# Staging the output projection's weights in the recurrent branch instead of the gating branch (two-layer hybrid trunk, one core)

## The chip, the cores and the metric

The kernel runs on one core of a Trainium2 chip. The metric is the device time of one launch in microseconds (us), the median of several runs. TensorE is PE in the profile, VectorE is DVE, ScalarE is ACT, GpSimd is POOL, and SyncE, which here only issues transfers, is SP.

## The reference

Two layers of the same form act on x, 1024 tokens by 1024 features in fp32. With h = RMSNorm(x) and one input projection `proj = h @ w_in` each layer computes three branches:

```python
ya = rg_lru(causal_depthwise_conv(xa, conv_w, conv_b), ...) * silu(ga)   # recurrent, 384 wide
yb = mla(q_lat, kv_lat, k_rope, positions, ...) * silu(gb)               # attention, 384 wide
yc = spatial_gating(u, v, ...) * silu(gc)                                # gating, 256 wide
y  = concatenate([rms_norm(ya, g[:384]), rms_norm(yb, g[384:768]), rms_norm(yc, g[768:])])
x  = x + rms_norm(y @ w_out, post_g)
```

The recurrent branch runs a convolution of width 4 along the tokens, two sigmoid gates per head and the linear recurrence `h[t] = a[t] h[t-1] + b[t]`. The gating branch multiplies u with a mix of the normalised v inside blocks of 128 tokens.

## The kernel before, in words

Every matrix product is done at fp32 accuracy with three matmuls. Both operands are split in two parts, `hi` (a rounded copy, made on ACT) and `lo` (what the copy misses, a subtraction on DVE or POOL); `mm3` (L126 to L128) adds hi·hi, hi·lo and lo·hi into one PSUM bank. So each weight takes the same road: a transfer from HBM into a slot (SP, L377 for w_in), the `hi` copy on ACT (L386), the `lo` subtraction on POOL or, for the u and v weights, on DVE (L387).

Slots come from a pool called `FS`: seven tiles F_136 to F_142, each 128 x 1024, and the rows of the tile Y while the branch that owns them does not need them. `take` hands out the slot that has been free longest in the program's text; a transfer into a re-used slot waits until the last reader of that slot is done, and SP issues its transfers in order, so one that waits for its slot holds up all that stand behind it.

A layer runs in this order. **Recurrent stage**: `group(g, half)` computes 256 features of xa and ga for one half of the tokens, runs the convolution (ACT L446, DVE L451 and L454) or the gate (ACT L422, DVE L424), and calls `drain(3)`, which issues three pending steps of the recurrence (`lru_steps`: DVE L485 to L509, ACT L473 to L492; the scan is L504). **u and v tokens**: eight tiles of 128 tokens against 512 columns in four weight parts, Gelu on ACT (L687, L690), statistics on DVE (L688). **Gate tokens**: eight tiles against 256 columns (ACT L717, DVE L718). **Latents**: eight tiles against 352 columns, then the gate of the attention branch (ACT L422, DVE L424), loading and scaling the weights w_uq (SP L821, DVE L824). **Attention**, then the **output projection**.

The output projection needs w_out in hi and lo form. `stage_wo` prepares all eight pieces of 128 x 1024 early: load to a slot (SP, L626), for k of 5 or more a scaling on ACT (L630), the split (ACT L367, POOL L368), and two stores to HBM buffers, `wo_dram`: hi on ACT's queue (L632), lo on POOL's queue (L633). The attention loads them back later.

Inside these stages a scheduler chooses each engine's order from its own cost estimates; each engine then runs its list in that order.

Of the kernel before, what the change touches and what calls it, by code (L numbers as in the profile page):

```python
# [8 lines left out]
F32R = mybir.dt.float32r  # L9
BF16 = mybir.dt.bfloat16  # L10
I32 = mybir.dt.int32
AF = mybir.ActivationFunctionType
# [12 lines left out]
W_ROWS = (0, 128, 256, 768, 896, 384, 512, 640)  # L25
# [64 lines left out]
def trunk_kernel(tc, A, out):  # L90
    nc = tc.nc
    keep = tc.keep_in_program_order
    V, S_, G, PE = nc.vector, nc.scalar, nc.gpsimd, nc.tensor
# [20 lines left out]
    def bank(kind):  # L114
        turn[kind] = (turn[kind] + 1) % len(banks[kind])
        return banks[kind][turn[kind]]
# [38 lines left out]
    par = cst.tile([128, 80], F32, name="par")  # L155
# [13 lines left out]
    FS = Slots(cst, NF, 1024, F32, "F")  # L169
# [8 lines left out]
    wo_dram = [[dram.tile([128, 1024], F32, name=f"wo{k}{c}") for c in "hl"] for k in range(8)]  # L178
# [187 lines left out]
    def split(src, h, lo, eng=None):  # L366
        S_.activation(h, src, AF.Copy)  # L367
        (eng or G).tensor_tensor(out=lo, in0=src, in1=h.bitcast(F32), op=ALU.subtract)  # L368
# [148 lines left out]
    def drain(n=1):  # L517
        for _ in range(n):
            if pend:
                pend.pop(0)()  # L520
# [39 lines left out]

    for l in range(DEPTH):

        xc, last, gw = {}, [], []

        def group(g, half):
            pss = [bank("PF") for m in range(2)]
            if g == 0:

                for p in range(2):
                    for m in range(2):  # L570
                        feat(pss[m], hT, ws[g], m, half, slice(p * 256, (p + 1) * 256))
            for m in range(2):
                f = 2 * g + m
                ps = pss[m]
                if g:
                    feat(ps, hT, ws[g], m, half)
                if f < 3:
                    if half == 0:
                        xc[f] = FS.take((128, 1024))
                    conv(l, f, half, ps, xc[f])  # L580
                    if half == 1:
                        steps = lru_steps(l, f, xc[f], gw)
                        pend.extend(steps[:-1])
                        last.append(steps[-1])
                else:
                    gate_in(ps, YA + f - 3, half)
                drain(3)
                if l == 0 and (g, half, m) == (0, 1, 0):
                    softplus_consts()
            if half == 1:  # L590
                ws[g].give()
# [24 lines left out]
        pend.extend(last)  # L616
        pend.append(lambda: [RS.give(t) for t in gw])

        staged = {}

        def stage_wo(n):

            k, r = n // 2, W_ROWS[n // 2]
            if n % 2 == 0:
                staged[k] = FS.take((128, 1024)), FS.take((128, 1024))
                nc.sync.dma_start(out=staged[k][0], in_=A["w_out"][l, r:r + 128, :])  # L626
                return
            st, hi = staged.pop(k)
            if k >= 5:
                S_.activation(st, st, AF.Copy, scale=bgain(r // 128))  # L630
            split(st, hi.bitcast(F32R), st.bitcast(F32R), G)
            S_.dma_start(out=wo_dram[k][0], in_=hi)  # L632
            G.dma_start(out=wo_dram[k][1], in_=st)  # L633
            FS.give(st)
            FS.give(hi)


        for r in yrow[3:5]:
            FS.retire(r)
        vg, ug, gg = [], [], []  # L640

        def bgain(j):
            return par[:, 48 + l * 8 + j:49 + l * 8 + j]

        sg = HS.take((128, 2, 256))
        nc.sync.dma_start(out=sg[:, 0], in_=A["sgu_norm_g"][l].partition_broadcast(128))
# [34 lines left out]
        for t in range(NT):  # L681
            if t % 4 == 0:
                vg.append(FS.take((128, 4, 256)))
                ug.append(FS.take((128, 4, 256)))
            ps = toks(hT, w, t, 512, "P8")
            v = vg[t // 4][:, t % 4]
            S_.activation(v, ps[:, 256:512], AF.Gelu_apprx_tanh)  # L687
            V.bn_stats(out=bst[:, t], in_=v)  # L688
            V.bn_aggr(out=mv[:, t], in_=bst[:, t])
            S_.activation(ug[t // 4][:, t % 4], ps[:, 0:256], AF.Gelu_apprx_tanh)  # L690
            if t == 3:
                pend.extend([lambda: sgu_norm(0), lambda: sgu_affine(0)])
            drain(2)
            stage_wo(t)
        w.give()
        drain(100)
        sw = HS.take((128, 4, 128))
# [14 lines left out]
        for t in range(NT):  # L712
            if t % 4 == 0:
                gg.append(FS.take((128, 4, 256)))
            ps = toks(hT, w, t, 256, "PK")
            th = HS.take((128, 256))
            S_.activation(th, ps[:, 0:256], AF.Tanh, scale=0.5)  # L717
            V.scalar_tensor_tensor(out=gg[t // 4][:, t % 4], in0=th, scalar=1.0, in1=ps[:, 0:256],  # L718
                                   op0=ALU.add, op1=ALU.mult)
            HS.give(th)  # L720
            drain(2)
            stage_wo(8 + t)
        w.give()
        drain(100)
        HS.give(sg)
# [46 lines left out]
        for t in range(NT):  # L772
# [16 lines left out]
            r = rsqrt(ms, 2)  # L789
# [3 lines left out]
            if t % 4 == 3:  # L793
                half = t // 4
                hs = slice(half * 512, (half + 1) * 512)
                for b in range(3):
# [8 lines left out]
                    for r0, n, h, r1, lo in todo:  # L805
                        hi = h[r0:r0 + n, hs]
# [32 lines left out]
        st = FS.take((128, 768))  # L839
# [224 lines left out]
        for n in range(len(units)):  # L1064
# [4 lines left out]
            if n >= len(units) - 4 and n % 2:  # L1069
                half = units[n][1] // 2  # L1070
# [18 lines left out]
        for t in range(NT):  # L1089
# [12 lines left out]
            r = row_rsqrt([z], cols)  # L1102
# [5 lines left out]
            if l + 1 < DEPTH:  # L1108
# [5 lines left out]
                else:  # L1114
# [5 lines left out]
                    n = YS.take((128, 2, 512))  # L1120
# [31 lines left out]
```

## Time and profile before

| | |
|---|---|
| median of 3 runs | 922.84 us (922.6 to 928.7) |
| the profiled execution | 925.49 us, span 923.7 us |
| PE busy | 874.6 us (95%) |
| DVE, ACT, POOL busy | 567.4, 519.5, 426.3 us (61, 56, 46%) |
| mean granted TensorE clock | 0.986 |
| moved over DMA | 86.92 MB |

PE busy 95% of the span leaves 49 us in which it does nothing. In the page's table of 40 slices of 23.1 us POOL shows 0 in the fourth and fifth (69 to 115 us) and in the 23rd and 24th (508 to 554 us): these lie in the recurrent stages of the two layers.

### The profile page before, as it was taken

How to read it: one execution, taken by the hardware profiler on the slowest of the kernel's cores; microseconds unless marked ns; L12 is line 12 of the kernel's file. 1: busy time of each engine (PE TensorE's matmuls, PEld its weight loads, DVE VectorE, ACT ScalarE, POOL GpSimd, SP SyncE). 2: the span in 40 equal slices, each digit the busy share in tenths (PEclk: the TensorE clock that was granted, in tenths of full speed). 3: DMA queues.
4: the chain of work that ended last, by engine and by line, in shares of the span. 5: the costliest groups of instructions: out<-in, count | busy, mean ns of one | idle time of the engine just before them, and what ended most of it. 6: DMA issues, size and time to landing. Idle time of an engine off the chain costs nothing. (4 is left out here: it accounts for less than half of the span.)

```text
span 923.7 us, 13488 instructions
## 1 busy us (share of the span) xinstructions
PE 874.6 (95%) x4982; PEld 768.2 (83%) x4982; DVE 567.4 (61%) x1096; ACT 519.5 (56%) x1032; POOL 426.3 (46%) x469
## 2 busy tenths in 40 slices
PE   4999998999999999989998999999989999899896
PEld 3998787998889888878897888899968888888786
DVE  4567955555599986444465687265446889854322
ACT  6447745554687787445442595353457778755212
POOL 4720056673055767365641002775312467636822
PEclk9999999999999999999999999999989999999998
DMA  7201465412001432123350043762100026201322
GB/s 275 55 25 46 112 220 190 157 64 61 12 1 47 135 126 83 46 71 114 134 152 18 23 111 133 251 222 70 42 7 1 1 58 217 92 23 47 125 103 92
DMA packets 45078, 86.92 MB, mean 94 GB/s; under 512 B 8824, under 2 KB 26836, under 8 KB 45012
## 3 DMA queue, kind: packets, MB, share of 16 engines
q1 hardware_dynamic: 35796, 52.50, 18.5%
q0 software_dynamic: 6912, 25.17, 7.9%
q10 hardware_dynamic: 2304, 8.39, 2.3%
q8 instruction: 39, 0.64, 0.3%
q14 instruction: 27, 0.22, 0.1%
HBM read 60.88 MB, written 25.17 MB: 93 GB/s over the span
## 5 line engine op out<-in xcount | busy, mean ns | idle before, releaser
L126 PE MATMUL pw<-R,R 128*128 128x512 f32 (+1 forms) x704 | 259.7, 370 | 9.4 <-ACT F L1006 3.2
L128 PE MATMUL pw<-R,R 128*128 128x512 f32 (+1 forms) x704 | 252.6, 360 | 1.5 <-POOL R L387 0.8
L127 PE MATMUL pw<-R,R 128*128 128x512 f32 (+1 forms) x704 | 253.1, 360 | 0.0
L126 PE MATMUL pa<-R,R 128*128 128x512 f32 (+3 forms) x540 | 188.6, 352 | 8.5 <-DVE F L718 3.3
L127 PE MATMUL pa<-R,R 128*128 128x512 f32 (+3 forms) x540 | 186.9, 347 | 0.0
L128 PE MATMUL pa<-R,R 128*128 128x512 f32 (+3 forms) x540 | 186.5, 347 | 0.0
L126 PEld LDWEIGHTS pw<-R,R 128*128 128x128 f32 x704 | 134.7, 192 | 32.0 <-ACT F L942 5.9
L128 PEld LDWEIGHTS pw<-R,R 128*128 128x128 f32 x704 | 134.7, 192 | 20.6 <-POOL R L387 1.3
L127 PEld LDWEIGHTS pw<-R,R 128*128 128x128 f32 x704 | 135.0, 192 | 17.1
L126 PEld LDWEIGHTS pa<-R,R 128*128 128x128 f32 x540 | 103.0, 191 | 20.6 <-DVE F L718 3.5
L944 POOL TENSOR_SCALAR F<-F,ring 128x128 f32<-128x128 f32 (+3 forms) x96 | 71.9, 752 | 85.2 <-DVE ring L943 84.0
L128 PEld LDWEIGHTS pa<-R,R 128*128 128x128 f32 x540 | 102.6, 191 | 10.2
L127 PEld LDWEIGHTS pa<-R,R 128*128 128x128 f32 x540 | 103.2, 191 | 9.0
L368 DVE TENSOR_TENSOR R<-pa,R 128x512 fp32r<-128x512 f32 (+1 forms) x120 | 73.8, 629 | 20.9 <-ACT R L367 20.3
L942 ACT ACTIVATE F<-pw,ring 128x128 f32<-128x128 f32 (+3 forms) x96 | 71.0, 741 | 27.3 <-DVE ring L940 25.2
L940 DVE TENSOR_REDUCE ring<-pw 128x1 f32<-128x128 f32 (+3 forms) x96 | 71.7, 748 | 10.7 <-PE pw L128 10.1
L387 POOL TENSOR_TENSOR R<-F,R 128x1024 fp32r<-128x1024 f32 (+1 forms) x24 | 54.2, 2268 | 43.6 <-ACT R L386 43.5
L973 PE MATMUL pa<-R,R 128*128 128x256 f32 x480 | 72.9, 288 | 0.5 <-DVE R L368 0.3
L367 ACT ACTIVATE R<-pa 128x512 fp32r<-128x512 f32 (+1 forms) x120 | 62.9, 553 | 16.4 <-PE pa L964 15.0
L973 PEld LDWEIGHTS pa<-R,R 128*128 128x128 f32 x480 | 64.6, 190 | 3.8 <-DVE R L368 0.5
L964 PE MATMUL pa<-ident,F 128*128 128x128 f32 x432 | 64.4, 274 | 3.5 <-DVE R L368 3.2
L329 ACT ACTIVATE H<-F 128x1024 bf16<-128x1024 f32 (+2 forms) x33 | 31.5, 954 | 55.5 <-DVE F L1008 28.1
(305 smaller groups left out, 1338.7 us busy)
## 6 DMA issues: line engine op xcount, KB each, us to landing
F<-in_w_in SPq DMA_DIRECT2D x24, 512.0 KB, 4.7
F<-in_x SPq DMA_DIRECT2D x13, 512.0 KB, 4.6
F<-in_w_out SPq DMA_DIRECT2D x9, 512.0 KB, 3.5
F<-x SPq DMA_DIRECT2D x8, 512.0 KB, 4.4
Y<-in_w_out SPq DMA_DIRECT2D x7, 512.0 KB, 3.4
x<-F SPq DMA_DIRECT2D x7, 512.0 KB
out_y<-F SPq DMA_DIRECT2D x7, 512.0 KB
Y<-in_w_in SPq DMA_DIRECT2D x6, 512.0 KB, 3.7
```

The source lines that it names most:

```text
L126: PE.matmul(ps, lhsT=sh, rhs=mh, start=start, stop=False)
L127: PE.matmul(ps, lhsT=sh, rhs=ml, start=False, stop=False)
L128: PE.matmul(ps, lhsT=sl, rhs=mh, start=False, stop=stop)
L329: order(S_.activation(q.bitcast(BF16)[:, c], xs[i % len(xs)].rearrange("p a b -> p (a b)")[:, c], AF.Square, scale=1.0 / 32, accum_out=ms[ ...
L367: S_.activation(h, src, AF.Copy)
L368: (eng or G).tensor_tensor(out=lo, in0=src, in1=h.bitcast(F32), op=ALU.subtract)
L387: self.eng.tensor_tensor(out=lo, in0=st, in1=h.bitcast(F32), op=ALU.subtract)
L940: V.tensor_reduce(out=mx, in_=sv, axis=AX.XY, op=ALU.max, negate=True)
L942: S_.activation(p[:, 0:n].rearrange("p (a b) -> p a b", a=sv.shape[1]), sv, AF.Exp, bias=mx, accum_out=sm)
L944: G.tensor_scalar(out=p[:, 0:n], in0=p[:, 0:n], scalar1=rs, scalar2=1.0, op0=ALU.mult, op1=ALU.mult)
L964: PE.transpose(pv[:, c, i * 128:(i + 1) * 128], p[i][:, b * 128:(b + 1) * 128], ident)
L973: PE.matmul(o, lhsT=sv, rhs=pt[:, part, c * 256:(c + 1) * 256], start=(b == 0 and part == 0), stop=(b == nb - 1 and part == 1))
```

## The change

`stage_wo` moves. Before, it is called after each of the eight u and v tokens and after each of the eight gate tokens: the even calls take two slots and load a piece, the odd calls split and store it. Now it is called in `group`, behind `drain(3)`, for nine calls per layer: call n splits and stores piece n-1 and loads piece n. One slot is held from a call to the next; the slot for hi is taken only when the split is issued. `bgain` moves up so that `stage_wo` can use it. No arithmetic is added or left out.

```diff
-        xc, last, gw = {}, [], []
+        xc, last, gw, staged = {}, [], [], []
...
+        def stage_wo(n):
+
+            if staged:
+                k, st = n - 1, staged.pop()
+                hi = FS.take((128, 1024))
+                if k >= 5:
+                    S_.activation(st, st, AF.Copy, scale=bgain(W_ROWS[k] // 128))
+                split(st, hi.bitcast(F32R), st.bitcast(F32R), G)
+                S_.dma_start(out=wo_dram[k][0], in_=hi)
+                G.dma_start(out=wo_dram[k][1], in_=st)
+                FS.give(st)
+                FS.give(hi)
+            if n < 8:
+                staged.append(FS.take((128, 1024)))
+                nc.sync.dma_start(out=staged[0], in_=A["w_out"][l, W_ROWS[n]:W_ROWS[n] + 128, :])
...
                 drain(3)
+                n = 4 * half + 2 * g + m - 1 if g < 2 else 7 + 2 * half + m
+                if 0 <= n <= 8:
+                    stage_wo(n)
...
-        staged = {}
-
-        def stage_wo(n):
-            k, r = n // 2, W_ROWS[n // 2]
-            if n % 2 == 0:
-                staged[k] = FS.take((128, 1024)), FS.take((128, 1024))
-                nc.sync.dma_start(out=staged[k][0], in_=A["w_out"][l, r:r + 128, :])
-                return
-            st, hi = staged.pop(k)
...
             drain(2)
-            stage_wo(t)
...
             drain(2)
-            stage_wo(8 + t)
```

Three places show how the instructions move. In the changed kernel the scaling of a piece is L574, the stores are L576 and L577, the load is L582, and the lines behind move by one (L687 is L688, L824 is L823).

**ACT, layer 0, end of the recurrent stage.** The `hi` copies of the last two u and v weight parts are `R_104<-F_141` and `R_133<-F_137` before, `R_133<-F_142` and `R_106<-F_139` after. Before:

```order
L386 ACTIVATE R_104<-F_141 128x1024
L473 ACTIVATE F_142<-pa_66,hb 128x512
L422 ACTIVATE H_143<-pa_67 128x512
L386 ACTIVATE R_133<-F_137 128x1024
L473 ACTIVATE Y<-pa_65,hb 128x512
L492 ACT_TABLE_LOAD
```

After:

```order
L367 ACTIVATE F_142<-F_139 128x1024
L473 ACTIVATE F_141<-pa_66,hb 128x512
L574 ACTIVATE F_140<-F_140,par 128x1024
L576 DMA wo5h<-F_142 128x1024
L492 ACT_TABLE_LOAD
L492 ACTIVATE Y<-Y 128x1024
L367 ACTIVATE Y<-F_140 128x1024
L422 ACT_TABLE_LOAD
L422 ACTIVATE H_144<-pa_68 128x512
L576 DMA wo6h<-Y 128x1024
L386 ACTIVATE R_133<-F_142 128x1024
L367 ACTIVATE Y<-Y 128x1024
```

The slot F_142 first holds the hi half of piece 5, must be stored, and is then loaded with the third weight part; the last gate of the stage (`H_144<-pa_68`) stands ahead of that copy now and behind it before.

**SP, start of layer 1.** The transfers around the last stores of layer 0's result (`x_146`), and the weights of the second feature group. Before:

```order
L377 DMA F_136<-in_w_in 128x4x256
L377 DMA F_142<-in_w_in 128x4x256
L1106 DMA x_146<-F_137 128x512 x2
L377 DMA F_139<-in_w_in 128x4x256
```

After:

```order
L377 DMA Y<-in_w_in 128x4x256
L582 DMA F_137<-in_w_out 128x1024
L582 DMA Y<-in_w_out 128x1024
L377 DMA F_140<-in_w_in 128x4x256
L1105 DMA x_146<-F_142 128x512 x2
L377 DMA F_136<-in_w_in 128x4x256
L377 DMA F_141<-in_w_in 128x4x256
```

The second group's two parts (F_136 and F_142 before, F_136 and F_141 after) now stand behind the last stores, and two loads of w_out stand ahead of them.

**DVE, layer 1, end of the latents.** `L424 Y<-H_143,pa_67` frees a PSUM bank; the scaling of the second piece of w_uq (F_137) is L824 before and L823 after. Before:

```order
L824 TENSOR_SCALAR F_137<-F_137,par 128x6x96
L368 TENSOR_TENSOR R_109<-F_139,R_109 128x512
L787 TENSOR_TENSOR F_136<-rt 128x32
L825 TENSOR_TENSOR F_137<-F_137 128x6x16
L424 SCALAR_TENSOR_TENSOR Y<-H_143,pa_67 128x512
```

After:

```order
L786 TENSOR_TENSOR F_136<-rt 128x32
L424 SCALAR_TENSOR_TENSOR Y<-H_143,pa_67 128x512
L787 TENSOR_TENSOR F_136<-F_136 128x16
L823 TENSOR_SCALAR F_137<-F_137,par 128x6x96
L824 TENSOR_TENSOR F_137<-F_137 128x6x16
```

The gate stood behind the scaling and stands ahead of it now.

## Rows read from the trace of the kernel before

**Rows 1.** The page's first part, the line of the engines: busy us, share of the span, instructions.

```profile
PE 874.6 (95%) x4982; PEld 768.2 (83%) x4982; DVE 567.4 (61%) x1096; ACT 519.5 (56%) x1032; POOL 426.3 (46%) x469
```

**Rows 2.** What PE waited for, in four stretches: the first two rows are of 110 to 170 us, the next two of 450 to 500, then one of 550 to 645 and one of 645 to 700. Columns: the awaited instruction, us in total, times, longest us.

```profile
PE pa L126 <- DVE F L718: 3.3, 1, 3.3
PE pw L126 <- ACT F L690: 1.2, 1, 1.2
...
PE pa L126 <- DVE R L358: 1.6, 1, 1.6
PE pw L128 <- POOL R L387: 0.8, 1, 0.8
...
PE pw L126 <- DVE R L368: 2.6, 1, 2.6
...
PE pa L126 <- DVE Y L424: 2.6, 2, 1.8
```

**Rows 3.** Busy time of each engine in stretches. Columns: stretch, its length, then PE, PEld, DVE, ACT and POOL busy us (with counts), the granted clock, the DMA share, GB/s.

```profile
60.00:120.00 60.00, 58.77 (x264) 48.46 (x264) 52.90 (x95) 40.68 (x48) 0.00 (x0) 1.00 0.22 62
...
150.00:155.00 5.00, 2.98 (x25) 2.77 (x24) 2.94 (x5) 2.38 (x7) 4.85 (x5) 1.00 0.29 113
155.00:160.00 5.00, 3.74 (x23) 3.74 (x24) 4.70 (x18) 1.15 (x1) 1.79 (x3) 0.77 0.66 211
160.00:165.00 5.00, 5.00 (x31) 5.00 (x31) 4.97 (x13) 2.68 (x5) 0.00 (x0) 0.88 0.43 105
...
500.00:560.00 60.00, 60.00 (x299) 51.07 (x298) 43.67 (x53) 37.44 (x44) 0.00 (x0) 1.00 0.23 62
...
595.00:600.00 5.00, 3.73 (x32) 3.53 (x30) 0.22 (x1) 3.54 (x7) 5.00 (x4) 1.00 0.41 135
600.00:605.00 5.00, 3.71 (x18) 3.71 (x19) 2.23 (x6) 3.26 (x6) 4.83 (x5) 0.66 0.47 158
...
670.00:675.00 5.00, 1.59 (x9) 1.25 (x10) 4.57 (x13) 3.44 (x10) 3.88 (x4) 0.82 0.08 19
675.00:680.00 5.00, 5.00 (x13) 3.95 (x12) 1.29 (x4) 0.37 (x1) 0.00 (x0) 0.50 0.00 0
```

**Rows 4.** The timeline of SP, ACT and DVE around layer 0's gate tokens. Columns here and in every timeline below: start us, us, engine, line, operation, out<-in, count, and in brackets the idle time before it and what ended it.

```profile
140.20 7.74 SPq L377 DMA_DIRECT2D F<-in_w_in  x2
...
150.70 0.79 ACT L386 ACTIVATE R<-F 128x704 fp32r<-128x704 f32 x1 [0.69 <-DMA F<-in_w_in]
...
153.16 1.43 DVE L268 CAST ring<-pos_i 128x8 f32<-128x8 int32 x1
...
155.80 0.41 DVE L718 SCALAR_TENSOR_TENSOR F<-H,pa 128x256 f32<-128x256 f32 x1
```

**Rows 5.** The chain of waits from 580 to 610 us, in layer 1's gate tokens. Columns: start us, us, what.

```profile
588.58 4.05 DMA wo3l<-Y
...
592.64 5.00 DMA Y<-in_w_out
...
600.54 0.70 DVE R L368
```

**Rows 6.** The timeline of SP and DVE at the end of layer 1's latents.

```profile
667.60 1.22 SPq L821 DMA_DIRECT2D F<-in_w_uq  x2
...
671.37 1.50 DVE L824 TENSOR_SCALAR F<-F,par 128x576 f32<-128x576 f32 x1 [0.43 <-DMA F<-in_w_uq]
...
673.67 0.67 DVE L424 SCALAR_TENSOR_TENSOR Y<-H,pa 128x512 f32<-128x512 f32 x1
```

**Rows 7.** What the handling of a piece of w_out costs: the first POOL instruction after the recurrent stage of layer 0, and ACT's split and scaling.

```profile
124.83 4.93 POOL L368 TENSOR_TENSOR F<-F,F 128x1024 fp32r<-128x1024 f32 x2 [67.96 <-ACT F L367]
...
597.74 1.06 ACT L367 ACTIVATE Y<-Y 128x1024 fp32r<-128x1024 f32 x1 [1.46 <-DMA Y<-in_w_out]
...
601.15 1.15 ACT L630 ACTIVATE F<-F,par 128x1024 f32<-128x1024 f32 x1 [0.36 <-DMA F<-in_w_out]
```

**Rows 8.** DVE's first scan of layer 0, PE's last matmul of the recurrent stage before the u and v tokens and the one behind it, and from the page's list of transfers the time from issue to landing (last column) of a part of w_in and a piece of w_out.

```profile
90.93 2.28 DVE L504 TENSOR_TENSOR_SCAN F<-Y,F 128x1024 f32<-128x1024 f32 x1
...
98.68 0.39 PE L128 MATMUL pa<-R,R 128*128 128x512 f32 x1
98.91 0.39 PE L126 MATMUL pa<-R,R 128*128 128x512 f32 x1
...
F<-in_w_in SPq DMA_DIRECT2D x24, 512.0 KB, 4.7
...
F<-in_w_out SPq DMA_DIRECT2D x9, 512.0 KB, 3.5
```

**Rows 9.** The timeline of SP and ACT at the start of layer 1: the issue of the second feature group's two parts, the issue behind the last stores, and the copy that waits for that one.

```profile
466.40 8.38 SPq L377 DMA_DIRECT2D F<-in_w_in  x2
...
477.25 0.40 SPq L377 DMA_DIRECT2D F<-in_w_in  x1
...
483.22 1.06 ACT L386 ACTIVATE R<-F 128x1024 fp32r<-128x1024 f32 x1 [3.35 <-DMA F<-in_w_in]
```

**Rows 10.** One DVE operation (L661, two inputs from SBUF) twice, in layer 0 and in layer 1, and the POOL split that runs beside the first.

```profile
140.15 2.39 POOL L368 TENSOR_TENSOR F<-F,F 128x1024 fp32r<-128x1024 f32 x1 [0.41 <-ACT F L367]
...
141.28 2.34 DVE L661 TENSOR_TENSOR Y<-Y,H 128x1024 f32<-128x1024 f32 x1
...
584.79 1.23 DVE L661 TENSOR_TENSOR F<-F,H 128x1024 f32<-128x1024 f32 x1
```

More of the change, by code (lines that the diff above doesn't have):

```diff
@@ L561, in trunk_kernel, with bgain @@
     for l in range(DEPTH):
-        xc, last, gw = {}, [], []
+        xc, last, gw, staged = {}, [], [], []
+        def bgain(j):
+            return par[:, 48 + l * 8 + j:49 + l * 8 + j]
+        def stage_wo(n):
[12 more added lines that the diff above has]
+                nc.sync.dma_start(out=staged[0], in_=A["w_out"][l, W_ROWS[n]:W_ROWS[n] + 128, :])
         def group(g, half):
@@ L617, in trunk_kernel @@
         pend.append(lambda: [RS.give(t) for t in gw])
-        staged = {}
-        def stage_wo(n):
-            k, r = n // 2, W_ROWS[n // 2]
-            if n % 2 == 0:
-                staged[k] = FS.take((128, 1024)), FS.take((128, 1024))
-                nc.sync.dma_start(out=staged[k][0], in_=A["w_out"][l, r:r + 128, :])
-                return
-            st, hi = staged.pop(k)
[L629 to L635, printed above, removed]
         for r in yrow[3:5]:
@@ L640, in trunk_kernel @@
         vg, ug, gg = [], [], []
-        def bgain(j):
-            return par[:, 48 + l * 8 + j:49 + l * 8 + j]
         sg = HS.take((128, 2, 256))
```

## The prediction

> **What bounds the kernel now.** I read the page's first part first: PE is busy 874.6 us, 95% of the span [rows 1]. So a change to the staging of w_out can only win in the 49 us in which PE stands idle, and in what those stops cost in clock afterwards. Then I read what PE waited for [rows 2]. Around the stages that the change touches there are three stops of some size: 3.3 us for L718 (layer 0, gate tokens), 2.6 us for L368 (layer 1, gate tokens) and 2.6 us in two waits for L424 (layer 1, latents). There are small ones where the recurrent stages begin or end: 1.2 us for L690, 0.8 and 1.6 us at layer 1's start. The table of stretches [rows 3] then tells each stop's whole price: a stretch of 5 us in which PE is busy less than 5 us, and the stretches behind it in which the granted clock is below 1. Last, the timelines and the chain tell what came late.
>
> **What the change removes.** *Layer 0, gate tokens.* PE is idle 5 - 2.98 = 2.02 us and 5 - 3.74 = 1.26 us, and then the clock is 0.77 and 0.88 in two stretches of 5 us, 5 x 0.23 + 5 x 0.12 = 1.75 us [rows 3]. Together 5.0 us. The cause is a late weight: SP waited 7.74 us at 140.20 for the slots of two latent parts, slots that pieces of w_out held; ACT, in order, stood at that part's copy until 150.70, and L718 came at 155.80, behind a cast of 1.43 us [rows 4]. In the changed kernel no piece of w_out is in this stage, and in SP's list the latent parts stand right behind the last u and v part. I book all of it: -5.0.
>
> *Layer 1, gate tokens.* Idle 1.27 and 1.29 us, then clock 0.66 for 5 us, 1.7 us [rows 3]: 4.3 us. The chain runs from the store of wo3's lo over the load of the next piece (issued 592.64, 5.00 us) through ACT to DVE L368 at 600.54, which PE awaits [rows 5]. Every link is w_out staging: -4.3.
>
> *Layer 1, latents.* Idle 5 - 1.59 = 3.41 us, then 0.82 and 0.50 of the clock, 0.9 + 2.5 = 3.4 us [rows 3]: 6.8 us. DVE's L424 at 673.67 stands in DVE's list behind L824, which waits for a transfer issued at 667.60 and starts at 671.37 [rows 6]. The third order excerpt has L424 ahead of that scaling: -6.8. This one is a by-product of the scheduler's new order, not of the work moved.
>
> The three give **-16.1 us**. Late next in the gate tokens would be the plain Gelu and tanh work, which has no transfer in it.
>
> **What it adds to the recurrent stages.** Per layer, eight hi copies of 1.06 and three scalings of 1.15 on ACT are 8.5 + 3.5 = 12 us; eight splits of about 2.4 on POOL are 19 us (the first row has two in 4.93) [rows 7]. POOL has room: it did nothing for 67.96 us there [rows 7]. ACT is busy 40.7 of 60 us in layer 0 and 37.4 in layer 1 [rows 3], so 12 more fit on average, and cost only where they stand ahead of something that PE needs.
>
> *a. Layer 0, start of the u and v tokens.* The first order excerpt shows the third weight part in the slot of piece 5's hi half. That slot comes free after the first scan (90.93 + 2.28 = 93.2 [rows 8]); some 2.7 us later now, because hi copies and a scaling stand ahead on ACT, an estimate from three hi copies less what ACT has free [rows 7]: 95.9. Then the hi copy 1.06, the wait behind the next piece's load (3.5 [rows 8]) and scaling (1.15) to about 101, the store (4.05, as wo3l took [rows 5]) to 105, the load of the part (4.7 [rows 8]) to about 110, its copy to 111. The fourth part's copy stands behind one more hi copy and one gate step: about 113.6, and its lo half, behind a step of the recurrence on DVE, 2 us later. PE begins the u and v tokens near 99, one matmul of 512 columns every 0.23 us [rows 8]; by its list 54 of them need only the first two parts, 12.3 us, so it arrives at about 111.2. I estimate waits of 2.4 us for the copy and 2.0 for the lo half, where 1.2 was [rows 2]: +3.2. A wait of that size cost 1.7 us of clock in layer 1 [rows 3]; I add 1.7. Bounds: 0, if PE's own progress is as late, and 7.3 + 1.7 = 9.0 if the fourth part slips by another store of 4.05. I take **+4.9**, nearer the middle, since the chain is long but each link has a row.
>
> *b. The same in layer 1.* The order is the same, but by the same sum the parts come just in time, since the scan lies earlier before the tokens. Bounds 0 and 3 (a's 3.2); I take **+0.5**.
>
> *c. Start of layer 1.* The second feature group's two parts were issued at 466.40; now they stand behind the last stores, as the transfer issued at 477.25 does now, whose copy began at 483.22 [rows 9]. Copy 1.06 and a POOL subtraction of 2.4 put the lo half at 486.7; PE would need it at about 483. That is a stop of some 3.75 us instead of 2.4 (0.8 and 1.6 [rows 2]): +1.3, and 1.8 of clock, as behind the 3.3 us stop: **+3.1**. Bounds: -0.8, if the old 0.8 goes, and +5.5, if the 1.6 stays as well and the clock is lost in full.
>
> *d. Start of layer 0.* Two pieces are split ahead of the weights of the third group. PE's next banks leave a margin of a few us there, so I take **+0.5**; bounds 0 and 3 (one POOL split of 2.4 plus its issue).
>
> *e. DVE beside POOL.* One DVE operation, L661, took 1.23 us alone and 2.34 beside a POOL split: 140.15 + 2.39 = 142.54 is where the split ends, and 142.54 + 1.1 is where L661 ends [rows 10]. DVE did nothing for itself until POOL was done. In the stage that now gets the splits DVE is busy 52.9 of 60 us in layer 0, mostly on operations of that kind, where it shared with nobody before. At the end of layer 0's stage, two splits (4.8 us) fall on DVE while a and its late copies leave it some 3 us idle: I take **+1.5**, between 0 and 4.8.
>
> Loads, stores and issues are the same in number; nothing waits for the stores until the attention.
>
> **The sum.** -16.1 + 4.9 + 0.5 + 3.1 + 0.5 + 1.5 = -5.6 us. The profiled execution of 925.49 becomes 919.9. It lies 2.65 above the median of the runs; the change carries over, and 922.84 - 5.6 = **917 us**.
>
> **The rivals.**
> *All new work is covered.* The stops of a, c and e don't appear, since POOL and ACT have the room that [rows 3, 7] show: 922.84 - 16.1 = 907. For it: PE did not wait once in 500 to 560, where it is busy 60.00 us [rows 3]. Against: the excerpts put late transfers ahead of needed weights.
> *The stops only move.* Costs at the upper ends of a to c with d (9.0 + 3 + 5.5 + 0.5 = 18.0) eat the gain: 922.84 - 16.1 + 18.0 = 925. For it: a 4.05 us store and a 4.7 us load in a row ahead of the part that PE needs.
> *DVE becomes the bound in the recurrent stage (slower).* Six splits of layer 0 after 60 us and eight of layer 1 are 14 x 2.4 = 33.6 us, if each blocks DVE as in [rows 10]. DVE's idle time is 7.1 and 16.3 us in the two stretches [rows 3], so 14.4 - 7.1 = 7.3 and 19.2 - 16.3 = 2.9 us come late even if every idle moment absorbs them; with 1.7 of clock per layer +13.6, in place of e's 1.5: 917 - 1.5 + 13.6 = 929. If half of the 33.6 reaches PE, 16.8 + 3.4 gives 936. I price it at 933; it turns the sign once more than 5.6 + 1.5 = 7.1 us of DVE's delay reach PE. Against: the convolution's operations and the gates read PSUM, and the recurrence may run late into the u and v tokens without PE waiting for it. Beside this stands a rule: the Trainium skill, page "SBUF — State Buffer", section "Who interferes with whom", has a DVE instruction with two SBUF inputs and a GpSimd instruction that reads SBUF exclude each other for the whole of the first. L661's stretch of 1.11 us agrees. By that rule the scans and products of the recurrence are all exposed, and the sum would be this rival's; my own sum takes only the splits that meet a DVE with PE close behind it.
> *The change doesn't do what it says.* The order excerpts show the move, so only the L424 by-product could fail; without its 6.8 us and with the rest as forecast 924, which falls in with the second rival.
>
> **Chances.** The forecast (911 to 921) 0.44; all covered 0.18; the stops move 0.20; DVE bound 0.18. I call 1% (913.6 and 932) what a measurement of this kernel can tell from no change. Faster: 0.18, and the forecast's lower part, 0.18, together 0.36. Slower: the upper part of the DVE rival, 0.12. Within: 0.52. The range of 906 to 930 leaves out about half of the first rival and half of the DVE rival, near 0.2.
>
> **What would show it.** Right: no wait of PE for L718 or for L368 in the gate tokens, none for L424 at the latents' end, clock 1.00 there; PE waiting in layer 0 near 111 for R<-F copies of w_in (L386, L387), and at layer 1's start for L387 for about 3.7 us. Wrong: DVE operations of 1.2 us taking 2 to 3.6 us in 60 to 120 with PE waiting for L424, L451 or L368 in the recurrent stage (the DVE rival); the u and v tokens starting without a wait (all covered); a wait for L424 at the latents still there (the by-product). The price that I know least is a.

## The result, and the profile after

The change makes the kernel slower: 932.0 us (median of 20 runs, 928.2 to 936.6) against 927.3 (20 runs, 921.5 to 938.3; the first three of these are the runs that the prediction had). The ratio is 1.0055, with a 95% interval of 1.0034 to 1.0076. Forecast were 917 us and a gain of 5.6. Of the 15 us between forecast and result, 4.5 lie in the start (the median of 20 runs before is 927.3, that of the three runs was 922.8) and 10.3 in the change (+4.7 in place of -5.6).

The page and the list of cores of the changed kernel, beside [rows 1]:

```profile
PE 877.2 (94%) x4982; PEld 766.1 (82%) x4982; DVE 589.8 (63%) x1096; ACT 522.3 (56%) x1033; POOL 428.3 (46%) x469
...
core 0: 932.5 us, clock 0.988
```

The profiled span is 8.8 us longer than before. DVE is busy 22.4 us longer (589.8 against 567.4), although it has the same 1096 instructions to do. That is the first hint. The second is a landmark: one matmul near the end of layer 0's attention waits 0.7 us for a POOL lo half in both kernels, and one in layer 1's output projection waits 2.6 us in both. Before and after, PE's timeline:

```profile
392.16 0.50 PE L128 MATMUL pw<-R,R 128*128 128x512 f32 x1 [0.71 <-POOL R L368]
...
872.42 0.50 PE L126 MATMUL pw<-R,R 128*128 128x512 f32 x1 [2.64 <-ACT F L1006]
```

```profile
408.31 0.50 PE L128 MATMUL pw<-R,R 128*128 128x512 f32 x1 [0.70 <-POOL R L368]
...
881.22 0.50 PE L126 MATMUL pw<-R,R 128*128 128x512 f32 x1 [2.64 <-ACT F L1005]
```

At the first landmark the changed kernel is 16.15 us late, at the second 8.8. So **layer 0 loses 16.2 us and layer 1 wins 7.4**. Layer 1 did what was forecast; layer 0 did not. A landmark is read from one execution: the two profiled ones lie 8.8 us apart, the medians 4.7, so a difference of 2 us between landmarks tells little.

A third landmark divides layer 0's loss: PE's first matmul of the latents (128x352), at 159.99 us before and at 165.78 in the change, with 757 and 754 matmuls ahead of it. From there to the first landmark:

```profile
159.99:392.16 232.17, 229.26 (x1424) 206.40 (x1423) 159.90 (x363) 152.16 (x349) 121.67 (x155) 1.00 0.22 73
```

```profile
165.78:408.31 242.53, 232.15 (x1428) 206.42 (x1427) 168.12 (x379) 148.88 (x345) 113.84 (x148) 1.00 0.17 53
```

So 5.8 us are lost ahead of the latents and 10.4 behind, in the rest of the gate tokens, the latents and the attention, where the changed kernel stages no piece of w_out in layer 0. There PE also has another order. Before, the first three matmuls of 128x384 (at 253.84 us) are followed by 24 of 128x512 into pa; in the change (at 265.72 us) five of these follow, then six into pw, and the 24 stand behind.

Layer 1's gate tokens and latents, beside [rows 3] (same columns; the work comes 9 to 16 us later on the clock of the span):

```profile
580.00:700.00 120.00, 119.97 (x718) 109.42 (x717) 64.07 (x146) 55.71 (x131) 40.60 (x41) 1.00 0.12 31
```

PE is busy all the time, at a granted clock of 1.00. The stops for L368 and L424 are gone.

Layer 0's recurrent stage, beside the row of 60 to 120 us in [rows 3]: the whole, and the last stretches of 5 us.

```profile
60.00:130.00 70.00, 61.37 (x267) 49.13 (x266) 58.06 (x88) 42.06 (x49) 16.80 (x11) 0.98 0.50 169
...
115.00:120.00 5.00, 2.44 (x9) 1.16 (x7) 5.00 (x2) 1.64 (x2) 3.55 (x2) 1.00 0.42 169
120.00:125.00 5.00, 2.42 (x6) 1.95 (x7) 3.63 (x4) 2.16 (x3) 0.00 (x0) 0.76 0.90 287
125.00:130.00 5.00, 5.00 (x22) 4.09 (x21) 1.32 (x4) 3.04 (x5) 0.00 (x0) 0.90 0.15 51
```

From 60 to 130 us PE stands idle 8.6 us (five stops: 0.46, 1.98, 1.06, 1.37, 3.76) where it stood 1.2 before, and then loses 5 x 0.24 + 5 x 0.10 = 1.7 us of clock. DVE's row from 115 to 120 is the one to look at: it is busy all 5.00 us with two instructions. DVE (its first scan first) and POOL there:

```profile
98.28 2.29 DVE L504 TENSOR_TENSOR_SCAN F<-F,F 128x1024 f32<-128x1024 f32 x1
...
102.20 2.88 DVE L485 TENSOR_SCALAR Y<-Y 128x1024 f32<-128x1024 f32 x1
...
108.85 2.78 DVE L491 TENSOR_SCALAR Y<-F 128x1024 f32<-128x1024 f32 x1
...
115.67 4.46 DVE L504 TENSOR_TENSOR_SCAN F<-Y,F 128x1024 f32<-128x1024 f32 x1
...
101.75 2.77 POOL L368 TENSOR_TENSOR F<-F,F 128x1024 fp32r<-128x1024 f32 x1 [29.30 <-ACT F L367]
...
108.62 2.46 POOL L368 TENSOR_TENSOR F<-F,Y 128x1024 fp32r<-128x1024 f32 x1 [3.23 <-ACT Y L367]
...
114.55 3.43 POOL L368 TENSOR_TENSOR Y<-Y 128x1024 fp32r<-128x1024 f32 x1 [2.60 <-ACT Y L367]
```

L485, L491 and the second scan each start while a POOL split runs, and end 0.55 to 2.2 us after it: as I read it, each waits for the split, and then runs its own time. Before, L485 and L491 took 0.68 and 0.69 us and the scan 2.28 [rows 8]:

```profile
110.88 0.68 DVE L485 TENSOR_SCALAR Y<-Y 128x1024 f32<-128x1024 f32 x1
...
117.99 0.69 DVE L491 TENSOR_SCALAR Y<-Y 128x1024 f32<-128x1024 f32 x1
```

The three splits of pieces 5 to 7 cost DVE 2.2 + 2.1 + 2.2 = 6.5 us. SP and ACT show the other half of the story:

```profile
102.31 6.67 SPq L377 DMA_DIRECT2D F<-in_w_in  x3
...
83.49 1.15 ACT L574 ACTIVATE Y<-Y,par 128x1024 f32<-128x1024 f32 x1 [4.80 <-DMA Y<-in_w_out]
...
104.06 1.16 ACT L574 ACTIVATE F<-F,par 128x1024 f32<-128x1024 f32 x1 [1.81 <-DMA F<-in_w_out]
...
122.56 1.27 ACT L473 ACTIVATE F<-pa,hb 128x512 f32<-128x512 f32 x2 [5.00 <-DVE R L387]
```

The last two u and v weight parts are issued at 107.48 and 108.61, within the first row (its first issue is not one of them), behind waits for slots; before, they were issued at 89.06 and 93.24. ACT stands 4.80 and 1.81 us at the scaling of pieces that have not landed, with the recurrence behind it in its list; and it stands 5.00 us at the recurrence's third gate, because the slot that it writes is still held by a weight part whose lo half DVE has not made yet.

Three theories came out of these rows. **Theory 1**: ACT's waits for w_out make the recurrence late. **Theory 2**: POOL's splits hold DVE up. **Theory 3**: pieces 5 to 7 keep the slots that the weight parts need.

### The profile page after: what moved, and what is told of

Same layout as the page of the kernel before. It is cut to its first block, busy times and chain, and to the rows that moved or that the text cites. A ratio compares the mean times of both kernels' runs of the same rounds, so it can differ in the third digit from the quotient of the medians.

```text
span 932.5 us, 13497 instructions
## 1 busy us (share of the span) xinstructions
PE 877.2 (94%) x4982; PEld 766.1 (82%) x4982; DVE 589.8 (63%) x1096; ACT 522.3 (56%) x1033; POOL 428.3 (46%) x469
## 4 chain that ended last, share of the span: by engine, by line
PE 45%; DVE 5%; POOL 2%; ACT 2%; issue 1%; DMA 1%; DVEq 0%; POOLq 0%; SPq 0%; ACTq 0%
PE pw L126 8%; PE pw L128 8%; PE pw L127 8%; PE pa L126 5%; PE pa L128 5%; PE pa L127 5%; PE pa L972 3%; PE pa L963 2%; DVE ring L939 1%; DVE R L368 1%; POOL R L368 1%; DMA F<-in_w_in 1%; PE pa L351 1%; POOL R L387 1%; DVE Y L504 0%
## 5 line engine op out<-in xcount | busy, mean ns | idle before, releaser
L126 PE MATMUL pw<-R,R 128*128 128x512 f32 (+1 forms) x704 | 259.8, 371 | 10.4 <-ACT F L941 3.5
L127 PEld LDWEIGHTS pw<-R,R 128*128 128x128 f32 x704 | 135.0, 192 | 22.4 <-DVE R L387 5.0
L368 DVE TENSOR_TENSOR R<-pa,R 128x512 fp32r<-128x512 f32 (+1 forms) x120 | 74.0, 630 | 23.6 <-ACT R L367 22.7
L387 POOL TENSOR_TENSOR R<-F,R 128x1024 fp32r<-128x1024 f32 (+1 forms) x20 | 45.6, 2291 | 45.5 <-ACT R L386 45.5
```

Source lines behind the costliest of these rows:

```text
L126: PE.matmul(ps, lhsT=sh, rhs=mh, start=start, stop=False)
L127: PE.matmul(ps, lhsT=sh, rhs=ml, start=False, stop=False)
L387: self.eng.tensor_tensor(out=lo, in0=st, in1=h.bitcast(F32), op=ALU.subtract)
```

## The experiments

All are compared with the kernel before by ratio, and with the changed kernel by the landmarks. Lateness below is that of the first matmul of the latents against 159.99 and, for all of layer 0, that of the first landmark against 392.16. The last column tells whether PE's order behind the latents is that of the kernel before (old: 24 matmuls of 128x512 behind the first three of 128x384) or that of the change (new: five).

| run | what differs from the changed kernel | us | ratio to before, 95% | late at the latents | layer 0 late | PE's order |
|---|---|---|---|---|---|---|
| the change | | 932.0 | 1.0034 to 1.0076 | +5.8 | +16.2 | new |
| e3 | layer 0: hi and scaling read a tile that is always there | 936.4 | 1.0076 to 1.0139 | +3.5 | +19.0 | new |
| e4 | layer 0: no lo subtraction | 929.3 | 0.9991 to 1.0039 | +2.6 | +12.1 | new |
| e7 | layer 0: subtraction on DVE | 920.9 | 0.9892 to 0.9954 | +3.5 | +5.1 | old |
| e8 | layer 0: POOL fills with zeros instead | 923.9 | one run | +1.8 | +7.7 | new |
| e14 | layer 0: pieces 2 to 7 on DVE | 928.2 | 0.9999 to 1.0047 | +0.4 | +12.3 | new |
| e12 | layer 0 as before the change | 917.5 | 0.9865 to 0.9945 | -1.7 | -1.3 | old |
| e13 | layer 0: pieces 5 to 7 in the u and v tokens | 915.3 | 0.9848 to 0.9899 | -0.8 | -1.4 | old |
| e15 | e13, and pieces 2 to 7 on DVE | 919.0 | 0.9876 to 0.9943 | +1.1 | +1.3 | old |

From the first matmul of the latents to the landmark the six kernels with the old order (before, e7, e11, e12, e13, e15) take 231.6 to 233.8 us, and the five with the new one 238.1 to 247.7. It is not lateness that costs this time: e14 reaches the latents 0.4 us late and then takes 244.06. That the order does is the nearest reading, but no run varies the order alone, so it is not shown.

Six kernels (e1, e2, e5, e6, e9, e10) carried a slip: a constant that I added was called `EARLY`, a name by which the kernel starts two tiles of the output projection early, inside the attention. They lost that early start in both layers, which has nothing to do with the change, and got PE stops of some 7 us at the end of layer 0's attention (e1 at 365 to 384 us: 1.54, 1.16, 0.58, 3.61). Their times are given, but none is held against a kernel without the slip; e12 and e13 repeat e1 and e5 without the slip.

**e1 and e12, layer 1 alone.**

```diff
-                if 0 <= n <= 8:
+                if l and 0 <= n <= 8:
...
+            if l == 0:
+                stage_old(t)        # the old stage_wo, in both token loops
```

> The staging moves to the recurrent branch in layer 1 only; layer 0 keeps the old places. The trace of the changed kernel is 16.1 us late at the output projection of layer 0 (408.31 against 392.16) and 8.8 us late at that of layer 1 (881.22 against 872.42), so layer 1 alone should win 7.3 us. Theory A (the loss sits in layer 0 alone, layer 1's gains are real): 0.8% faster than before, ratio 0.990 to 0.994, no stop at L368 in layer 1's gate tokens and none of L424 behind the latents. Theory B (the gains in layer 1 are an accident of the late start): within 0.2% of before or slower.

> Layer 1 alone moves, and the output projection starts early as in the kernel before. Theory A: layer 0's times are the kernel before's to within 1 us up to 390 us, and layer 1 wins 7.3 us: ratio to before 0.990 to 0.994. Theory B: within 0.2% of before.

e1 gave 923.7 us, ratio 0.996 (0.9934 to 0.9986), with the slip. e12 gave 917.5, 0.9905. Its landmarks:

```profile
390.88 0.50 PE L128 MATMUL pw<-R,R 128*128 128x512 f32 x1 [0.71 <-POOL R L368]
...
860.53 0.74 PE L126 MATMUL pw<-R,R 128*128 128x512 f32 x1 [2.64 <-ACT F L1028]
```

Layer 0 is as before (390.88 against 392.16); from one landmark to the next it takes 469.65 us, where before took 480.26 and the change 472.91. So layer 1 wins by itself, 10.6 us here; most of what it wins beyond the change's 7.4 is a stop of 2.5 us for L368 that the change has at 812 us and e12 has not. Theory A held: the loss sits in layer 0 alone.

**e2, layer 0 alone** (e1's edit with the layers exchanged).

> The staging moves in layer 0 only; layer 1 keeps the old places. Theory A: 16 us slower than before, ratio 1.013 to 1.018, and layer 1's stops of 2.6 us (L368) and 3.5 us (L424) are there again. Theory B: about as the changed kernel, ratio 1.004 to 1.008.

It took 946.7 us, ratio 1.0181 to 1.0247. The slip is in it, so the 1.013 to 1.018 expected can't be compared; but layer 1's old stops were back in its trace (2.82 us for L368, 1.81 for L424), and PE's stops up to 345 us are those of the change (1.95 for ACT L473, 3.68 for L387).

**e3, ACT never waits for w_out.**

```diff
-                if k >= 5:
-                    S_.activation(st, st, AF.Copy, scale=bgain(...))
-                split(st, hi.bitcast(F32R), st.bitcast(F32R), G)
+                src = st if l else hT[0][0][0]...     # a tile of h, always there
+                if k >= 5:
+                    S_.activation(st if l else hi, src, AF.Copy, scale=bgain(...))
+                S_.activation(hi.bitcast(F32R), src, AF.Copy)
+                G.tensor_tensor(out=st.bitcast(F32R), in0=st, in1=hi, op=ALU.subtract)
```

> The changed kernel, but in layer 0 the hi copy and the scaling of a piece read a tile of h that is always there (the value of hi is not w_out's; loads, stores, slots and the POOL subtraction stay). So ACT never stands in its list for a load of w_out. Theory 1 (ACT's waits of 2.53, 4.80 and 1.81 us for w_out make the recurrence late): the first scan of layer 0 starts by 93 us instead of 98.3, PE's waits for L473 (0.46, 1.98, 1.37) go, and the time is 4 to 8 us below the changed kernel. Theory 2 (POOL's splits hold DVE up): the scan stays late by 2 to 4 us, DVE's L485, L491 and the second scan keep their 2.9, 2.8 and 4.5 us, and the time changes by under 2 us. Theory 3 (the weight parts of the u and v tokens come late through the slots): PE's stop of 3.8 us for L387 stays, under 2 us.

The first half came true: ACT's waits went, the first scan started at 92.75, and PE's early stops went. The time did not fall. DVE, POOL (its split is L577 here), ACT and PE of this run:

```profile
92.75 2.29 DVE L504 TENSOR_TENSOR_SCAN F<-F,F 128x1024 f32<-128x1024 f32 x1
...
110.89 3.19 DVE L509 SCALAR_TENSOR_TENSOR Y<-F,Y 128x1024 f32<-128x1024 f32 x1
114.00 1.21 DVE L387 TENSOR_TENSOR R<-F,R 128x1024 fp32r<-128x1024 f32 x1
...
109.63 3.37 POOL L577 TENSOR_TENSOR Y<-Y 128x1024 fp32r<-128x1024 f32 x1 [3.85 <-ACT Y L576]
...
115.39 0.69 ACT L473 ACTIVATE F<-pa,hb 128x512 f32<-128x512 f32 x1 [4.90 <-DVE R L387]
...
116.12 0.79 PE L126 MATMUL pa<-R,R 128*128 128x512 f32 x1 [6.01 <-ACT F L473]
```

A recurrence that is 5.5 us earlier waits at the same place: ACT needs the slot that the weight part holds until DVE's L387, and L387 stands behind L509, which a POOL split holds. PE stands idle 6.8 us from 60 to 130 us instead of 8.6, but behind the one stop of 6.01 us the granted clock falls to 0.84, 0.50 and 0.64 in three stretches of 5 us, 5.1 us where the change lost 1.7. At the first matmul of the latents e3 is still 2.3 us ahead of the change, and it loses that and 2.9 more behind it. So theory 1's waits are real, but taking them away alone doesn't bring layer 0 back.

**e4, e7, e8, e14: no POOL split beside DVE in layer 0.** Four ways: leave the subtraction out; do it on DVE; let POOL fill the tile instead, which reads nothing; do pieces 2 to 7 on DVE.

```diff
-                split(st, hi.bitcast(F32R), st.bitcast(F32R), G)
+                S_.activation(hi.bitcast(F32R), st, AF.Copy)                                 # e4, l == 0
+                split(st, hi.bitcast(F32R), st.bitcast(F32R), G if l else V)                 # e7
+                S_.activation(hi.bitcast(F32R), st, AF.Copy); G.memset(st, 0.0)              # e8, l == 0
+                split(st, hi.bitcast(F32R), st.bitcast(F32R), V if l == 0 and k >= 2 else G) # e14
```

> The changed kernel without POOL's subtraction of the eight pieces in layer 0 (their lo half is left out: the piece itself is stored in its place). Slots come free some 2.4 us sooner per piece. Theory 2: DVE's L485, L491 and second scan go back to 0.7, 0.7 and 2.3 us, which takes 6.5 us off DVE's list at the end of the recurrent stage; PE's stop for L387 falls from 3.8 us to under 1.5, and the time is 4 to 7 us below the changed kernel. Theory 1: the first scan still starts near 98, PE still waits for L473, and the time is under 2 us below. Theory 3: only the earlier slots tell, 1 to 2 us below.

> The changed kernel with the subtraction of layer 0's eight pieces on DVE (about 1.2 us each) instead of POOL (2.4). Theory 2: a POOL split beside DVE costs DVE up to 2.4 us, so doing the work itself is no dearer; L485, L491 and the scans take 0.7, 0.7 and 2.3 us, and the time is the changed kernel's or up to 3 us less. If DVE's own time were the limit and POOL's splits free, 8 x 1.2 = 9.6 us more on DVE would make it 3 to 6 us slower than the changed kernel.

> The changed kernel with POOL filling the piece with zeros in layer 0 (a fill reads nothing) instead of the subtraction; the lo half is left out. If the hold is on what POOL reads, DVE's products of two SBUF tiles (L486, L496, L504) that meet a fill keep 1.2 and 2.3 us; if any POOL work in SBUF holds DVE, some of them are stretched by up to the fill's length.

> The changed kernel with layer 0's pieces 2 to 7 subtracted on DVE, 0 and 1 on POOL. The run with all eight on DVE (ratio 0.992) had a new stop of 4.3 us for L451 at 40 us, where DVE did pieces 0 and 1. Theory 2 (one cost, POOL's hold on DVE late in the stage): that stop goes, the rest stays as there: ratio 0.986 to 0.991. If the gain of that run came from elsewhere, 0.996 or more.

In all four the stretches of 2 us are gone (L485 took 1.03 us in e8). In e7, where DVE itself does eight subtractions more:

```profile
99.74 0.68 DVE L485 TENSOR_SCALAR Y<-Y 128x1024 f32<-128x1024 f32 x1
...
108.11 0.69 DVE L491 TENSOR_SCALAR Y<-F 128x1024 f32<-128x1024 f32 x1
...
118.59 2.28 DVE L504 TENSOR_TENSOR_SCAN F<-Y,F 128x1024 f32<-128x1024 f32 x1
```

Layer 0 got 4.1 us (e4), 11.1 (e7), 8.4 (e8) and 3.8 (e14) faster than in the change. All four signs speak for theory 2, that of e7 only just, but most of the gain of e7, the kernel in which DVE has more work of its own and which is 11 us faster, is not theory 2's. Ahead of the latents, where the splits are, e4 gains 3.2 us on the change, e7 2.3, e8 4.0 and e14 5.4. e14 is the better of e7 and e14 there, as I had expected: e7 has a new stop of 4.29 us at 40 us, where DVE does pieces 0 and 1. Behind the first matmul of the latents neither stages a piece, and there e7, with the old order, takes 10.3 us less than e14 with the new one:

```profile
163.46:397.21 233.75, 229.44 (x1428) 206.38 (x1427) 164.34 (x374) 148.21 (x345) 111.53 (x147) 1.00 0.18 55
```

```profile
160.42:404.48 244.06, 233.53 (x1428) 208.22 (x1427) 168.20 (x371) 149.69 (x346) 114.74 (x148) 0.99 0.17 52
```

By its time alone e14 (1.002) met the line that I had set for "the gain of that run came from elsewhere" (0.996 or more), and for most of that gain this is right. e4, 2.7 us below the change, is short of the 4 to 7 of theory 2 as well, and its interval and e14's touch that of the change. A scheduler orders each kernel anew, and with the hold gone a wait on slots is what is left: in e14 PE stops 3.32 us at 114.32 for ACT's L473, in e4 2.82 us for the copy of a weight part. e8's fills also took POOL 0.95 us instead of 2.4.

**e5 and e13, pieces 5 to 7 later in layer 0.**

```diff
-                if 0 <= n <= 8:
+                if 0 <= n <= (8 if l else 5):          # stage_wo(5) then splits piece 4 and loads nothing
...
+            if l == 0 and 1 <= t < 5:                  # in the u and v tokens
+                stage_wo(4 + t, False)
```

> The changed kernel, but in layer 0 only pieces 0 to 4 are staged in the recurrent branch; pieces 5 to 7 go to the u and v tokens 1 to 4. Theory 3 (the fourth u and v weight part waits for slots that pieces 5 to 7 hold: its transfer was issued at about 109 us, before the change at 93): that part is issued by 97, the stops at 112 to 123 us (1.06, 1.37, 3.76) and the clock loss behind them go, the third scan starts by 130 instead of 142, and the time is 6 to 10 us below the changed kernel, at or under the kernel before (ratio 0.992 to 1.000). Theory 1 (waits of ACT for w_out alone) gives 3 to 5 us, since the waits of 4.80 and 1.81 us are for pieces 6 and 5 to 7. Theory 2 (POOL holding DVE) gives 3 to 5 us as well; what tells them apart is whether ACT still stands in its list for a slot.

> Pieces 5 to 7 of layer 0 in the u and v tokens, early start as before. The stops at the end of layer 0's attention (1.5, 1.2, 3.3 us) should go, the one wait of 3.0 us for ACT at the start of the u and v tokens and a wait of 1.0 us for L718 should stay. Layer 0 then costs 0 to 3 us against the kernel before instead of 16, layer 1 wins 7: ratio 0.992 to 0.997. If the loss of layer 0 lay in the first five pieces, the ratio is 1.000 or more.

e5 (with the slip) gave 917.8 us, ratio 0.9852 to 0.9917; e13 gave 915.3, 0.9848 to 0.9899. Both are faster than their expected ranges. Layer 0 of e13 is 1.4 us ahead of the kernel before and **17.5 us ahead of the change**, 6.6 of it ahead of the latents and 11.0 behind, where PE has the old order again. SP, DVE and POOL of e13:

```profile
95.89 0.89 SPq L377 DMA_DIRECT2D F<-in_w_in  x2
...
111.86 2.29 DVE L504 TENSOR_TENSOR_SCAN F<-Y,F 128x1024 f32<-128x1024 f32 x1
...
129.49 2.39 POOL L368 TENSOR_TENSOR F<-F,F 128x1024 fp32r<-128x1024 f32 x1 [59.81 <-ACT F L367]
```

The last two u and v parts are issued from 95.89 on instead of at 107.48 and 108.61; POOL does no split for 59.81 us, while DVE runs the recurrence; the third scan starts at 124.81 instead of 142.38. The early pieces still hold DVE (L454 took 2.15 us at 61.83), and PE doesn't notice. One wait is left at the start of the u and v tokens, 2.79 us for a Gelu, and none in the gate tokens. So the whole loss of layer 0 goes when pieces 5 to 7 stand elsewhere: shown. How it divides between their slots, their splits and the order that the scheduler makes of the rest is not.

**e9, e10, e11 and e15: both remedies, and DVE in layer 1.** e9 is e5 with layer 0's subtractions on DVE, e10 the same with both layers', e11 the change with both layers' on DVE, e15 is e13 with pieces 2 to 7 of layer 0 on DVE.

> Both remedies in layer 0: pieces 5 to 7 in the u and v tokens, and layer 0's subtraction on DVE. If the two remove different costs (slots held by the last three pieces; POOL holding DVE for the first five), the time is 2 to 4 us below the better of them: ratio to before 0.984 to 0.988. If both remove the same cost (what the last three splits do to DVE), it equals the run with three pieces later: 0.986 to 0.991.

> The same with the subtraction on DVE in layer 1 as well. DVE is idle 16 of 60 us in layer 1's recurrent stage before the change, so a POOL split there costs PE little: theory 2 with slack gives a difference to the run before it of under 2 us; if layer 1 pays for the hold as layer 0 did, 3 to 6 us less.

> The changed kernel with the subtraction on DVE in both layers. Against the run with it in layer 0 alone (ratio to before 0.992) the same question: within 2 us if layer 1's DVE has room, 3 to 6 us less if it hasn't.

> Both: pieces 5 to 7 of layer 0 in the u and v tokens, pieces 2 to 7 on DVE. Two separate costs: 2 to 4 us under the better of e13 and e14, ratio 0.984 to 0.988. One cost: within 2 us of the better.

e15 gave 0.991 (0.9876 to 0.9943), no better than e13, which fits one cost for both remedies; it is 3.7 us slower than e13, where I had expected to be within 2. e9 (927.8, 0.9973 to 1.0014, with the slip) had a new stop of 5.27 us at 40 us, where DVE, busy with pieces 0 and 1, is late for the convolution; e7 has it with 4.3. e10 (933.1, 1.0036 to 1.0074) and e11 (925.0, 0.9937 to 0.9982) answer the question on layer 1 the other way than either line expected: its subtractions on DVE make it slower (e10 against e9, which share the slip; e11's interval overlaps e7's). From landmark to landmark e11 takes 477.3 us against 471.0 in e7, with a new stop of 2.61 us for L718 at 613 us. In layer 1 the splits are better left on POOL.

**e6, all of layer 0 in the u and v tokens, one piece per token.**

```diff
+            if l == 0:                                 # u and v tokens; nothing in the recurrent stage
+                stage_wo(t, False)
```

> Layer 1 as in the changed kernel; in layer 0 one piece per u and v token (the old place, but twice as fast and with one slot held between calls), so nothing of w_out is in layer 0's recurrent stage and nothing in its gate tokens. If layer 0's loss is in the recurrent stage and its gain in the gate tokens, both are had here: the stop for L718 of 3.3 us goes or falls under 1, the recurrent stage is as before, and the time is 10 to 14 us below the changed kernel, ratio to before 0.985 to 0.992. If POOL's splits are the harm wherever they stand, the u and v tokens get new stops and the ratio is 0.995 to 1.005.

936.2 us, ratio 1.0047 to 1.0109, with the slip, slower than either line expected. The recurrent stage was as before (PE idle 1.0 us from 60 to 130). But before the gate tokens PE stopped

```profile
162.72 0.96 PE L129 MATMUL pa<-R,R 128*128 128x352 f32 x2 [9.70 <-ACT R L389]
```

for a latent weight part that SP could issue only at 151 to 158 us, behind the pieces. It is the stop of [rows 4] again, three times as long. The slip doesn't reach this place. Here too the pieces' slots hold up a weight part that PE needs soon.

## Why the prediction was wrong

**What bounds, and the three stops to be removed.** Right for layer 1: the stops for L368 and L424 went with their clock, 11.1 us as booked. The reading was half wrong, though: of the 3.41 us before the latents' end L424 had 1.81, and for the rest PE waited for ACT's L755, in a row of the view of [rows 2] that I had passed over. This wait went too; one of 1.35 us like it came in layer 0's latents.

```profile
PE pw L754 <- ACT Y L755: 1.7, 1, 1.7
```

Right for layer 0's stop of 3.3 us for L718; but "late next would be the plain Gelu and tanh work, which has no transfer in it" was wrong. In its place PE waited 0.57 and 1.81 us for L718 at 172 to 176, so 2.4 of the 5.0 us came back. Ahead of the second L718 stands an operation of DVE that takes some 0.2 us by itself, beside a POOL split that has nothing to do with w_out:

```profile
172.47 2.33 DVE L284 TENSOR_SCALAR F<-F 128x128 f32<-128x128 f32 x1
...
172.34 2.37 POOL L368 TENSOR_TENSOR R<-F,R 128x1024 fp32r<-128x1024 f32 x1 [5.17 <-ACT R L367]
```

**b and c, layer 1.** c was booked with +3.1: the stops for the second group's parts are 0.56 + 1.71 = 2.3 us (2.4 before, 1.6 of them for L358), with 1.7 of clock behind them that wasn't there before, so about +1.5. b was booked with +0.5 and is 1.46 + 0.38 = 1.8, inside its bound of 3. All in all layer 1 was forecast at -4.3 - 6.8 + 0.5 + 3.1 = -7.5 and measured at -7.4 between the landmarks. That both agree to 0.1 us is luck: in e3, e4, e7, e8 and e12 to e15, whose layer 1 stages in the same places, it takes 468.2 to 472.3 us, 8 to 12 less than before.

**Layer 0: the steps that failed.** It was forecast at -5.0 + 4.9 + 0.5 + 1.5 = +1.9 and measured at +16.2.

*a and e, ahead of the latents.* Together they were booked with +6.4, of which e, DVE beside POOL, was 1.5. Between 60 and 130 us they cost 8.6 - 1.2 = 7.4 us of idle time and 1.7 of clock, 9.1. (d, booked with +0.5, cost 0.3 of idle time up to 60 us.) The first scan ended at 100.57 and not at 95.9, since ACT had waited for pieces. The copies of the two parts, expected to end at 111 and 113.6, ended at 112.70 and 117.56, and the last lo half, expected at 115.6, at 122.52. What the sum missed is that a and e feed each other. L387 of the last part stands behind a scan that a POOL split holds for 2.2 us, ACT's next gate needs the slot that this L387 frees, and the recurrence's next step needs that gate. I had priced each with the other absent, and called the 3 us that DVE waits in a a cover for e. I also took ACT's 12 us as work that "fits on average" and never asked whom its list would hold while it waits for a piece to land (4.80 us at 83 us); e3 shows that this alone did not set the end. Less what the gate tokens gave back, layer 0 is 5.8 us late at the first matmul of the latents.

*Nothing, for the latents and the attention.* The larger miss is a term that isn't in the sum. Of the 16.2 us, 10.4 lie behind the first matmul of the latents: 7.5 of idle time, of which 2.4 are L718's, and 2.9 in which the profile counts PE as busy, with 1428 matmuls against 1424. The prediction rests on the two kernels' orders in three places, and says of the rest only that "nothing waits for the stores until the attention"; PE's order from there on is another. Which of its differences costs the time is open. e13, with the old order, takes 231.56 us there against 232.17 before.

**The rivals.** "DVE becomes the bound in the recurrent stage" came nearest, with 929 to 936 us and 0.18. That 932 lies in it is in part luck: its 6 to 13 us stood on 922.8, and the change cost 4.7 on 927.3. Its mechanism is in the traces, in layer 0 alone and for some 6 us at most: layer 1, whose DVE was idle 16.3 of 60 us [rows 3], won what was forecast, and the 10.4 us behind the latents are not in that rival either. "The stops only move" named a's chain of a store and a load in a row, and gave 925.

## What to carry to other kernels

An engine that stands idle in a stage is not free in it. Ask what its work will share with the busy one: here POOL's splits and DVE's recurrence. Then ask what the moved work holds while it waits, a slot or a place in a list and who is next for that: here three pieces stood in the slots of two weight parts. Where a scheduler orders each kernel anew, compare the orders of every stage, not only of those that the change touches. And where a change moves a list of pieces, try part of it: five of eight pieces in layer 0 and all in layer 1 (e13) beat both kernels, with 915 us.

## What the runs showed of the hardware

In these traces a DVE operation with two inputs in SBUF, or a tensor-scalar operation on tiles in SBUF, that starts during a POOL split waits for the split to end. In the changed kernel L454, which handles three columns in 0.21 us, took 2.19 us; POOL's split beside it:

```profile
62.56 2.19 DVE L454 SCALAR_TENSOR_TENSOR Y<-tails,par,Y 128x3 f32<-128x3 f32 x1
...
62.35 2.38 POOL L368 TENSOR_TENSOR F<-F,F 128x1024 fp32r<-128x1024 f32 x1 [1.93 <-ACT F L367]
```

Both end within 0.02 us of each other (64.75 and 64.73). So the price is what is left of POOL's operation, whatever the size of DVE's. The hold goes both ways: the split at 114.55, which started beside DVE's L387 (114.54, 1.22 us), took 3.43 us instead of 2.4. And not every DVE operation is held: three of L451, which reads PSUM and SBUF, ran in 2.31 us, 0.75 each as elsewhere, two of them beside a split, and the statistics of L689, with one input in SBUF, took 0.43 us beside one (e13, at 133.00) and as much without.

```profile
42.15 2.31 DVE L451 SCALAR_TENSOR_TENSOR F<-pw,par,F 128x511 f32<-128x511 f32 x3
...
42.56 2.40 POOL L368 TENSOR_TENSOR F<-F,Y 128x1024 fp32r<-128x1024 f32 x1
```

When POOL only fills (e8, POOL and DVE):

```profile
112.99 0.95 POOL L579 MEMSET Y<- 128x1024 f32 x1 [5.38 <-ACT Y L578]
...
113.16 2.28 DVE L504 TENSOR_TENSOR_SCAN F<-Y,F 128x1024 f32<-128x1024 f32 x1
...
98.57 0.95 POOL L579 MEMSET F<- 128x1024 f32 x1 [29.92 <-ACT F L578]
...
99.04 1.03 DVE L485 TENSOR_SCALAR Y<-Y 128x1024 f32<-128x1024 f32 x1
```

the scan, which reads two tiles and starts in the middle of a fill, keeps its 2.28 us, while L485, which reads one tile and writes it back, waits 0.34 us. The Trainium skill, page "SBUF — State Buffer", section "Who interferes with whom", says just this: operations with two SBUF inputs contend only with a GpSimd instruction that reads SBUF, while copies and tensor-scalar operations in their two-port modes contend with any. These rows agree with it, if L485 runs in such a mode, which no row shows.
